# Summing layer 0's modulation by products with ones, moving a step's activations ahead of copies, and giving half-size weights their own small buffers

## The chip, the cores and the metric

One Trainium2 chip, one of its cores. The metric is the device time of one execution in microseconds (us). The kernel before takes 1404.36 us (median of 3 runs).

## The reference, cut to what matters

Two layers run over 512 positions of 2048 features. Each begins with a modulation that comes from the conditioning vector `c` alone, and with a wide projection of the modulated, normalised activations:

```python
c_act = jax.nn.silu(c)
for l in range(2):
    mod = c_act @ w_ada[l] + b_ada[l]            # 2048 x 6144
    shift, scale, gate = jnp.split(mod, 3, axis=-1)
    h = _layernorm(x) * (1.0 + scale[:, None, :]) + shift[:, None, :]
    p = h @ w_in[l]                              # 2048 x 3904
    u_f, z_f, cq, ckv, k_r, z_a = jnp.split(p, split_pts, axis=-1)
    # Fourier mixing of u_f, attention from cq, ckv, k_r, gates from z_f, z_a
    y = jnp.concatenate([y_f, y_a], axis=-1) @ w_out[l]
    x = _layernorm(DEEPNORM_ALPHA * x + gate[:, None, :] * y, ln_g[l], ln_b[l])
```

## The kernel before, in words

Every large product is split into a high and a low part of each operand (`split`: a cast on ScalarE, ACT, at L146, a subtraction on VectorE, DVE, at L147) and runs as three TensorE products (`mm3`, L150 to L152).

**Modulation.** `ada` goes over the rows of `w_ada`: a tile is loaded (L211), and DVE multiplies it by the conditioning values, one value for each partition, and adds it into `acc` (L244, L246). What is left is a sum over the 128 partitions. `finish` does it: each 128 x 128 block of `acc` is transposed on TensorE (L259, plain float32, against the identity), DVE sums along the free dimension (L260), and `ada_finish` adds the bias into `modT` (L220). `ada` is called 14 times in the two layers: six for the shift and scale of layer 0, two for its gate, six for layer 1. A block whose width is at most 512 has two halves in `acc`, and each half is transposed by itself. `finish` runs some units of weights later (`DL0`, `DLY`) or at the next step (`finish_late`).

**Layer 0's projection in steps.** All of `w_ada` would have to come before the first product, so layer 0 is cut into five steps of 1, 2, 3, 4 and 6 blocks of 128 features (`SZ`). A step needs only the shift and scale of its own blocks. In a step `make_h` modulates each block (an activation on ACT at L362, then `split`), and eight column groups follow (`k_group`, in the order of `FIRST`: UA, UB, CQ, CKV, two of ZF, two of ZA). UA keeps its own four PSUM banks (`pa`) over all steps. The other seven share the four banks of `pm`: in the first step their results are copied to SBUF sums by ACT (L1118), in later steps added to them by DVE (L1120). A bank is free for the next group when that is done. `finish` takes its banks from `pm` too: two for four or more blocks.

**Weights.** `Stream` loads ahead of use, up to four units, and converts two units ahead. A unit is two blocks of rows by up to 512 columns (512 KB), or one block where a step has an odd number (steps one and three, eight units each). `dense` gives every unit one of the three `wr` buffers (4 KB for each partition). The `t2` pool has nine buffers of 2 KB for each partition, for the modulated activations, rotary tables and other short-lived tiles. The loads are issued by the SP queue.

**Order.** The program is written in the order in which it should run, and a scheduler lays out each engine's queue: of the instructions that are ready by its own estimate, the one that stands first in the program goes first. On the chip each queue then runs in that order. `tc.high_priority(offset=n)` counts the instructions of a block as standing n places earlier. It moves nothing past its operands.

Of the kernel before, what the change touches and what calls it, by code (L numbers as in the profile page):

```python
# [9 lines left out]
F32 = mybir.dt.float32  # L10
# [3 lines left out]
ALU = mybir.AluOpType  # L14
AX = mybir.AxisListType
# [67 lines left out]
def trunk_kernel(ctx: ExitStack, tc: tile.TileContext, x, c, positions, w_ada, b_ada, w_in, q_norm,  # L83
# [8 lines left out]

    DL0, DLY = 2, 3

    KO = 2

    NE, HA = 5, 2
# [29 lines left out]
    def wraw(shape):  # L127
        return wrp.tile(shape, F32, tag="wr", name=nm("wr"))
# [4 lines left out]
    def sm(n, tag):  # L133
        return smp.tile([P, n], F32, tag=tag, name=nm(tag), bufs=4 if tag in ('mx', 'ssum') else 2)
# [4 lines left out]
    def pm():  # L139
        return psm.tile([P, 512], F32, tag="pm", name=nm("pm"))  # L140
# [36 lines left out]
    GP.dma_start(odd, odds)  # L177
    identr = const.tile([P, P], F32R, name="identr")
    V.tensor_copy(identr, ident)
    mhalf = const.tile([P, 4], F32, name="mhalf")  # L180
    V.memset(mhalf, -0.5)
    cact = const.tile([P, NK], F32, name="cact")
# [50 lines left out]
    def ada(l, pieces, cols, tiles=None):  # L233

        w = sum(n for _, n in pieces)
        nr = 1024 // w
        two = 2 if w <= 512 else 1
        acc = acp.tile([P, 1024], F32, tag="acc", name=nm("acc"))[:, :two * w].rearrange("p (a n) -> p a n", a=two)
        for r0 in range(0, NK, nr):
            t = tiles[r0 // nr] if tiles else ada_load(l, r0, nr, pieces)  # L240
            for r in range(r0, r0 + nr):
                a = acc[:, r % two]
                if r < two:
                    V.tensor_scalar(a, t[:, r - r0], cact[:, r:r + 1], None, op0=ALU.mult)  # L244
                else:
                    V.scalar_tensor_tensor(out=a, in0=t[:, r - r0], scalar=cact[:, r:r + 1], in1=a,  # L246
                                           op0=ALU.mult, op1=ALU.add)
            if r0 + nr < NK:
                yield

        def finish():
            red = sm(8, 'red')
            for i in range(0, w // P, 4 // two):
                ps = pm()
                n = min(4 // two, w // P - i)
                for j in range(n):
                    for a in range(two):
                        o = (j * two + a) * P
                        PE.transpose(out=ps[:, o:o + P], in_=acc[:, a, (i + j) * P:(i + j + 1) * P], identity=ident)  # L259
                V.tensor_reduce(red[:, i:i + n], ps[:, :n * two * P].rearrange("p (j q) -> p j q", j=n),  # L260
                                axis=AX.X, op=ALU.add)
            ada_finish(l, red[:, :w // P], *cols)
            if cols[0] == 40:
                ps = pm()
                PE.transpose(out=ps[0:16, 0:P], in_=modT[l][:, 32:48], identity=ident)
                row = t2([16, P])
                A.copy(row, ps[0:16, 0:P])
                SP.dma_start(gated[l:l + 1, :].rearrange("l (j q) -> (l j) q", q=P), row)

        late.append([DL0 if l == 0 and pieces[0][0] == SZ[0] * P else DLY, finish])  # L270
        yield
# [97 lines left out]

    def dense(src, row0, col0, n, nr=2):  # L370
        def load():
            t = wraw([P, nr, n])
            SP.dma_start(t, src[row0:row0 + nr * P, col0:col0 + n].rearrange("(r p) c -> p r c", p=P))
            return t

        def conv(t):
            h, l = big([P, nr, n]), big([P, nr, n])
            split(h, l, t)
            return h, l
        return Unit(load, conv)  # L380
# [273 lines left out]
    for l in range(DEPTH):  # L654
# [430 lines left out]
        if l == 0:  # L1085

            for step, (k0, nk) in enumerate(STEPS):
                final = k0 + nk == NK
                if step > 0:
                    finish_late()  # L1090
                for k in range(k0, k0 + nk) if step else ():
                    h[k] = make_h(0, xT[k // 2][:, k % 2], k)
                if final:
                    cw, dt = fourier_weights(0)
                left = [0 if final else float(sum(NK // (1024 // (256 * n)) for n in chunks(STEPS[step + 1][1])))]
                pace = left[0] / (8.0 * len(pairs(k0, nk)) * LEADS[step])

                def k_group(g, banks, work=lambda: None):
                    n = g[1]
                    k00, k01 = (0, NK) if g == UA else (k0, k0 + nk)  # L1100
                    for k, nr in pairs(k0, nk):
                        w = st.next()
                        p_ = min(pace, left[0])
                        left[0] -= p_
                        bg_step(p_ if p_ > 0 else ZL if final else ZP)
                        if g in ZF or g in ZA:
                            fm_half(banks, w, h, k, k == k00, k + nr == k01)
                        else:
                            tm_half(banks, w, h, k, n, k == k00, k + nr == k01)
                        work()  # L1110
                    if g == UA:
                        return banks
                    if k0 == 0:
                        sums[g] = [big([P, 2, n], F32) for _ in range(2)]
                    s_ = [sums[g][tb // 2][:, tb % 2] for tb in range(NT)]
                    for tb in range(NT):
                        if k0 == 0:
                            A.copy(s_[tb], banks[tb][:, :n])  # L1118
                        else:
                            V.tensor_tensor(s_[tb], s_[tb], banks[tb][:, :n], op=ALU.add)  # L1120
                    return s_

                if step == 0:
                    keep = [pa() for _ in range(NT)]
                if not final:
                    for i, g in enumerate(FIRST):
                        k_group(g, keep if g == UA else [pm() for _ in range(NT)])
                        if step == 0 and i == 3:
                            cos_t, sin_t = rotary_tables()
                    continue  # L1130

                def pas():
                    return [pa() for _ in range(NT)]

                def pieces(gen, then=iter(())):
                    def run():
                        next(then, None)
                        for _ in range(2):
                            next(gen, None)
                    return run  # L1140

                fa = fourier(0, folded(k_group(UA, keep)))
                pq = k_group(CQ, [pm() for _ in range(NT)])
                pkv = k_group(CKV, pas(), pieces(fa))
                lq = latent_q(pq)
                next(lq)
                ub = k_group(UB, pas(), pieces(fa, lq))
                drain(fa)
                lkv = latent_kv(pkv)
                next(lkv)  # L1150
                fb = fourier(1, folded(ub))
                for i, g in enumerate(ZF):
                    zs = k_group(g, pas(), pieces(fb, lkv))
                    silu(zs, zs)
                    if i == 0:
                        gate_f(0, zs)
                drain(fb)
                gate_f(1, zs)
                rq = rotary_queries(RN0)
                for i, g in enumerate(ZA):  # L1160
                    zs = k_group(g, pas(), runner(rq) if i else lambda: None)
                    silu(zs, zs)
                    spill(i, zs)
                    if i == 0:
                        next(rq)
        else:
            unfolded(first_group(), 0)
            st.ahead(4, UAH)
            with tc.issue_after(hold[0]):
                banks = fm_group(ada=G0)  # L1170
            unfolded(banks, H)
            cw, nq, dt = folded_constants(1)
            st.ahead(4, 2)
            fb = fourier_folded(u_pass())
            unfolded(fm_group(runner(fb, FW)), H + 4)
            drain(fb)
            gt = gates()
            lq = latent_q(tm_group(CQ, runner(gt)))
            drain(gt)
            next(lq)  # L1180
            lkv = latent_kv(tm_group(CKV, runner(lq), G1))
            next(lkv)
            rq = rotary_queries(1)

            def last():
                next(lkv, None)
                next(rq, None)

            next(rq)
            unfolded(fm_group(last, G1), 4)  # L1190
            drain(lkv)
# [160 lines left out]
```

## Time and profile before

| | us |
|---|---|
| median of 3 runs (lowest, highest) | 1404.36 (1404.01, 1406.08) |
| the profiled execution | 1404.26 |
| its span, first to last instruction | 1402.5 |
| TensorE busy | 1344.3 |
| VectorE busy | 1015.6 |
| ScalarE busy | 579.6 |

The span is the profiled time from the first instruction to the last. The 1.8 us around it belong to the time but not to any instruction. PE is TensorE's products, PEld its weight loads, which run beside the products. A queue with a q (SPq) is the issuing side of an engine. Products are pipelined: a record of 0.39 us is followed by the next one after about 0.23 us when nothing holds it.

### The profile page before, as it was taken

The page shows a single profiled execution, that of the slowest core. Times are in us where ns is not written, and L with a number is a line of the kernel's source. Part 1 is how long each engine was busy: PE and PEld are TensorE (multiplying, and loading weights), DVE is VectorE, ACT ScalarE, POOL GpSimd, SP SyncE. Part 2 cuts the span into 40 slices and gives each one's busy share as a digit, 9 for nine tenths or more (in the row PEclk, how much of TensorE's full clock was granted, in tenths as well). Part 3 has the DMA queues.
Part 4 walks back from the last instruction along what each step waited for, and adds up shares of the span by engine and source line. Part 5 has one row for each costly group of instructions (what it writes and reads, how often), then busy time and mean ns, then how long its engine had stood idle before and what let it go on. Part 6 is the DMA issues. An engine that isn't in the chain of part 4 may idle for free. (4 is left out here: it accounts for less than half of the span.)

```text
span 1402.5 us, 18691 instructions
## 1 busy us (share of the span) xinstructions
PE 1344.3 (96%) x6949; PEld 1141.2 (81%) x6949; DVE 1015.6 (72%) x1670; ACT 579.6 (41%) x1052; POOL 55.5 (4%) x82
## 2 busy tenths in 40 slices
PE   4899999999999999999988999998999999999996
PEld 3688888787888888788877888887898888888885
DVE  7899999849978986658588748567655576642448
ACT  6722332224437776112167524323234677721210
POOL 1000000000000000000030001011000000000001
PEclk9999999999999999999998999999999999999998
DMA  9988898824764444968336435369444221263323
GB/s 288 299 293 300 271 349 286 306 76 122 211 206 140 157 128 161 317 199 283 105 145 203 161 96 166 105 205 367 152 119 121 74 67 54 80 236 105 91 60 120
DMA packets 134546, 253.24 MB, mean 181 GB/s; under 512 B 19308, under 2 KB 50168, under 8 KB 134456
## 3 DMA queue, kind: packets, MB, share of 16 engines
q1 hardware_dynamic: 127416, 228.73, 50.1%
q0 software_dynamic: 7040, 23.34, 4.9%
q8 instruction: 54, 0.88, 0.3%
q14 instruction: 36, 0.29, 0.1%
HBM read 237.32 MB, written 14.70 MB: 180 GB/s over the span
## 5 line engine op out<-in xcount | busy, mean ns | idle before, releaser
L150 PE MATMUL pa<-b,b 128*128 128x512 f32 (+4 forms) x1432 | 537.4, 377 | 11.6 <-ACT b L146 5.5
L151 PE MATMUL pa<-b,b 128*128 128x512 f32 (+4 forms) x1432 | 535.9, 375 | 4.3 <-DVE ln_v L187 4.3
L152 PE MATMUL pa<-b,b 128*128 128x512 f32 (+4 forms) x1432 | 534.5, 374 | 1.9 <-DVE b L147 1.9
L146 ACT CAST b<-wr 128x1024 fp32r<-128x1024 f32 (+3 forms) x184 | 180.0, 988 | 356.1 <-PE pa L152 181.1
L150 PEld LDWEIGHTS pa<-b,b 128*128 128x128 f32 x1432 | 271.2, 190 | 59.7 <-ACT b L146 9.2
L151 PEld LDWEIGHTS pa<-b,b 128*128 128x128 f32 x1432 | 272.1, 190 | 48.1 <-DVE ln_v L187 4.6
L152 PEld LDWEIGHTS pa<-b,b 128*128 128x128 f32 x1432 | 271.5, 190 | 48.2 <-DVE b L147 2.9
L147 DVE TENSOR_TENSOR b<-wr,b 128x1024 fp32r<-128x1024 f32 (+3 forms) x184 | 208.1, 1141 | 136.5 <-PE pa L151 84.7
L246 DVE SCALAR_TENSOR_TENSOR acc<-ada,cact,acc 128x1024 f32<-128x1024 f32 (+2 forms) x193 | 227.2, 1184 | 23.1 <-DMA ada<-in_w_ada_dram 21.2
L150 PE MATMUL pm<-b,b 128*128 128x512 f32 (+3 forms) x594 | 201.7, 341 | 1.2 <-ACT b L146 0.8
L151 PE MATMUL pm<-b,b 128*128 128x512 f32 (+3 forms) x594 | 197.2, 333 | 0.0
L152 PE MATMUL pm<-b,b 128*128 128x512 f32 (+3 forms) x594 | 197.0, 333 | 0.0
L150 PEld LDWEIGHTS pm<-b,b 128*128 128x128 f32 x594 | 111.7, 189 | 17.8 <-ACT b L146 2.7
L151 PEld LDWEIGHTS pm<-b,b 128*128 128x128 f32 x594 | 112.3, 189 | 10.5
L152 PEld LDWEIGHTS pm<-b,b 128*128 128x128 f32 x594 | 112.2, 189 | 10.4
L146 ACT CAST b<-pm 128x512 fp32r<-128x512 f32 (+4 forms) x110 | 54.9, 530 | 72.6 <-PE pm L800 17.8
L147 DVE TENSOR_TENSOR b<-pm,b 128x512 fp32r<-128x512 f32 (+4 forms) x110 | 64.1, 610 | 23.6 <-ACT b L146 23.0
L1120 DVE TENSOR_TENSOR b<-b,pm 128x512 f32<-128x512 f32 (+1 forms) x88 | 55.5, 656 | 4.5 <-PE pm L152 4.1
L146 ACT CAST b<-t 128x512 fp32r<-128x512 f32 (+1 forms) x73 | 35.9, 525 | 31.4 <-PE pm L151 9.5
L1039 DVE TENSOR_REDUCE mx<-pa 128x1 f32<-128x512 f32 x64 | 42.9, 684 | 5.3 <-PE pa L1037 4.7
L1044 ACT ACTIVATE t<-t,ssum 128x512 f32<-128x512 f32 x64 | 45.9, 735 | 1.2 <-DVE ssum L1043 1.2
L1042 ACT ACTIVATE t<-pa,mx 128x512 f32<-128x512 f32 x64 | 44.0, 693 | 4.6 <-DVE mx L1039 4.5
(186 smaller groups left out, 1120.7 us busy)
## 6 DMA issues: line engine op xcount, KB each, us to landing
wr<-in_w_in_dram SPq DMA_DIRECT2D x105, 512.0 KB, 4.6
ada<-in_w_ada_dram SPq DMA_DIRECT2D x96, 512.0 KB, 5.3
wr<-in_w_out_dram SPq DMA_DIRECT2D x64, 512.0 KB, 4.1
ada<-in_w_ada_dram SPq DMA_DIRECT2D x96, 256.0 KB, 4.9
ada<-in_w_ada_dram POOLq DMA_DIRECT2D x32, 512.0 KB, 5.4
b<-in_x_dram SPq DMA_DIRECT2D x16, 512.0 KB, 6.3
ada<-in_w_ada_dram SPq DMA_DIRECT2D x32, 192.0 KB, 5.3
wr<-in_w_q_b_dram SPq DMA_DIRECT2D x48, 128.0 KB, 3.0
```

What stands on the lines that cost most here:

```text
L146: A.copy(hi, src)
L147: V.tensor_tensor(lo, src, f(hi), op=ALU.subtract)
L150: PE.matmul(o, lh, rh, start=first, stop=False)
L151: PE.matmul(o, lh, rl, start=False, stop=False)
L152: PE.matmul(o, ll, rh, start=False, stop=last)
L246: V.scalar_tensor_tensor(out=a, in0=t[:, r - r0], scalar=cact[:, r:r + 1], in1=a, op0=ALU.mult, op1=ALU.add)
L1039: V.reduce_max(mx, ps, axis=AX.X, negate=True)
L1042: A.activation(e, ps, AF.Exp, bias=mx, accum_out=ssum)
L1044: A.activation(e, e, AF.Copy, scale=ssum)
L1120: V.tensor_tensor(s_[tb], s_[tb], banks[tb][:, :n], op=ALU.add)
```

## The change

It has five edits.

1. `finish` uses no transposes and no reduction. Each block of `acc` is the stationary operand of a plain float32 product with a column of ones (`onec`, 128 x 1), two halves accumulate in PSUM, and `ada_finish` reads the sums from there. All 14 calls use it, in one PSUM bank each.
2. A unit of one row block goes into a `t2` buffer and not a `wr` buffer.
3. The `make_h` calls of a step stand 250 places earlier for the scheduler (`HP`).
4. In the first step, every second copy of the sums of the four ZF and ZA groups is on DVE and not on ACT (eight copies).
5. The column of ones is set once at the start.

```diff
+    HP = 250
...
+    onec = const.tile([P, 1], F32, name="onec")
+    V.memset(onec, 1.0)
...
         def finish():
-            red = sm(8, 'red')
-            for i in range(0, w // P, 4 // two):
-                ps = pm()
-                n = min(4 // two, w // P - i)
-                for j in range(n):
-                    for a in range(two):
-                        o = (j * two + a) * P
-                        PE.transpose(out=ps[:, o:o + P], in_=acc[:, a, (i + j) * P:(i + j + 1) * P], identity=ident)
-                V.tensor_reduce(red[:, i:i + n], ps[:, :n * two * P].rearrange("p (j q) -> p j q", j=n),
-                                axis=AX.X, op=ALU.add)
-            ada_finish(l, red[:, :w // P], *cols)
+            ps = pm()
+            for j in range(w // P):
+                for a in range(two):
+                    PE.matmul(ps[:, j:j + 1], acc[:, a, j * P:(j + 1) * P], onec, start=a == 0, stop=a == two - 1)
+            ada_finish(l, ps[:, :w // P], *cols)
...
-            t = wraw([P, nr, n])
+            t = wraw([P, nr, n]) if nr > 1 else t2([P, nr, n])
...
-                for k in range(k0, k0 + nk) if step else ():
-                    h[k] = make_h(0, xT[k // 2][:, k % 2], k)
+                with tc.high_priority(offset=HP):
+                    for k in range(k0, k0 + nk) if step else ():
+                        h[k] = make_h(0, xT[k // 2][:, k % 2], k)
...
                         if k0 == 0:
-                            A.copy(s_[tb], banks[tb][:, :n])
+                            if tb % 2 and (g in ZF or g in ZA):
+                                V.tensor_copy(s_[tb], banks[tb][:, :n])
+                            else:
+                                A.copy(s_[tb], banks[tb][:, :n])
```

## Rows read from the trace of the kernel before

**Rows 1.** The page's first part: busy us, share, instructions of each engine.

```profile
PE 1344.3 (96%) x6949; PEld 1141.2 (81%) x6949; DVE 1015.6 (72%) x1670; ACT 579.6 (41%) x1052; POOL 55.5 (4%) x82
```

**Rows 2.** Windows: stretch, its length, each engine's busy us, clock, DMA share, GB/s.

```profile
20.00:40.00 20.00, 16.25 (x89) 14.21 (x90) 18.39 (x42) 17.69 (x33) 0.17 (x1) 1.00 0.86 264
40.00:60.00 20.00, 16.56 (x78) 12.73 (x77) 14.75 (x22) 17.27 (x33) 0.00 (x0) 1.00 0.93 308
60.00:80.00 20.00, 18.63 (x90) 15.60 (x89) 19.51 (x26) 6.20 (x7) 0.00 (x0) 1.00 0.99 342
...
62.00:290.00 228.00, 227.84 (x1056) 190.70 (x1057) 213.79 (x262) 63.53 (x81) 2.95 (x5) 1.00 0.86 292
```

**Rows 3.** Timeline of PE, steps one to two: start us, us, instruction, idle before.

```profile
30.66 0.50 PE L150 MATMUL pa<-b,b 128*128 128x512 f32 x1 [1.58 <-ACT b L146]
...
46.28 0.30 PE L259 MATMUL pm<-ident,acc 128*128 128x128 f32 x1 [0.87 <-DVE acc L246]
46.85 0.98 PE L259 MATMUL pm<-ident,acc 128*128 128x128 f32 x7 [0.27 <-DVE acc L246]
...
54.03 0.50 PE L150 MATMUL pm<-b,b 128*128 128x512 f32 x1 [0.39 <-ACT b L1118]
...
58.91 0.50 PE L150 MATMUL pa<-b,b 128*128 128x512 f32 x1 [1.85 <-ACT b L146]
...
62.16 0.50 PE L152 MATMUL pa<-b,b 128*128 128x512 f32 x1 [1.37 <-DVE b L147]
```

**Rows 4.** Timeline of ACT around the start of step two.

```profile
50.07 0.82 ACT L362 ACTIVATE t<-xT,modT 128x512 f32<-128x512 f32 x1
...
56.24 2.09 ACT L1118 COPY b<-pm 128x512 f32<-128x512 f32 x4
58.15 1.23 ACT L146 CAST b<-t 128x512 fp32r<-128x512 f32 x2
```

**Rows 5.** Timeline of DVE: the modulation of steps one and two.

```profile
27.68 0.69 DVE L260 TENSOR_REDUCE red<-pm 128x2 f32<-128x512 f32 x1 [0.92 <-PE pm L259]
28.29 0.68 DVE L147 TENSOR_TENSOR b<-wr,b 128x512 fp32r<-128x512 f32 x1
28.89 0.16 DVE L220 TENSOR_TENSOR modT<-red,vecT 128x2 f32<-128x2 f32 x1
...
47.84 1.28 DVE L260 TENSOR_REDUCE red<-pm 128x2 f32<-128x512 f32 x2
...
49.64 0.16 DVE L220 TENSOR_TENSOR modT<-red,vecT 128x4 f32<-128x4 f32 x1
...
61.41 1.29 DVE L147 TENSOR_TENSOR b<-t,b 128x512 fp32r<-128x512 f32 x2
```

**Rows 6.** Groups by line: count, busy us, mean ns of one, idle before.

```profile
L260 DVE TENSOR_REDUCE red<-pm 128x4 f32<-128x512 f32 (+2 forms) x27 | 17.4, 675 | 3.6 <-PE pm L259 3.5
...
L259 PEld LDWEIGHTS pm<-ident,acc 128*128 128x128 f32 x106 | 12.5, 141 | 3.2 <-ACT b L1118 1.3 <-DVE acc L246 0.5
...
L1118 ACT COPY b<-pm 128x512 f32<-128x512 f32 (+1 forms) x28 | 14.6, 583 | 3.3 <-PE pm L152 2.9
...
L1120 DVE TENSOR_TENSOR b<-b,pm 128x512 f32<-128x512 f32 (+1 forms) x88 | 55.5, 656 | 4.5 <-PE pm L152 4.1
```

**Rows 7.** Timeline of PE: plain float32 products, six in the code at L554.

```profile
839.83 3.59 PE L554 MATMUL pm<-b,b 128*128 128x512 f32 x8
```

**Rows 8.** Timeline of PEld: weight loads of the same products, later in the same stretch.

```profile
843.88 0.30 PEld L554 LDWEIGHTS pm<-b,b 128*128 128x128 f32 x2 [0.19 <-PE pa L152]
```

**Rows 9.** Lines of that source: count of products, ns (min/median/max), first and last start.

```profile
L554 PE MATMUL pm<-b,b x12: 590/593/668, 839.8 to 845.3; 128*128 128x512 f32 x12
```

**Rows 10.** Timeline of the SP queue's issues.

```profile
19.78 0.43 SPq L211 DMA_DIRECT2D ada<-in_w_ada_dram  x1
25.21 0.33 SPq L373 DMA_DIRECT2D wr<-in_w_in_dram  x1
```

**Rows 11.** Waits from 36 to 64 us: total us, times, longest.

```profile
DVE acc L246 <- DMA ada<-in_w_ada_dram: 5.4, 6, 1.7
```

## The prediction

> **What bounds the kernel now.** I read the page's totals first, then the windows, then the timelines of the engines around layer 0's first steps, and then the rows of the instructions that are removed and added. TensorE is the bound: it is busy for 1344.3 of 1402.5 us, DVE for 1015.6 [rows 1]. The windows say where it is not. From 20 to 80 us it lacks 3.75, 3.44 and 1.37 us of each 20, and from 62 to 290 us, the rest of layer 0's steps, it lacks 0.16 of 228 us in all [rows 2]. DVE is at 94% in that stretch (213.79 of 228), but no product waits for it, so time taken off DVE there is worth nothing by itself, and time put on PE there is paid in full.
>
> The timeline of PE shows the one seam of the steps [rows 3]. The first product starts at 30.66. From 45 to 62 us PE stops five times: 0.87 and 0.27 us for `acc`, ahead of and between the transposes of step two's `finish`; 0.39 us for a copy of a sum that must free a `pm` bank; 1.85 us for the high part of step two's first `h`; 1.37 us for its low part. That is 4.75 us, and the windows from 40 to 80 us give 4.81 [rows 2]. The other engines say why the last two are so long. `modT` is there at 49.64 + 0.16 = 49.80 us [rows 5]. ACT does the first modulation at 50.07, but the cast to the high part only at 58.15, right behind the four copies of sums that start at 56.24, and DVE makes the low part at 61.41 [rows 4, 5]. So some 9 us go by in queues between operands that are ready and a cast of about 0.6 us.
>
> **Edit 1, the products with ones.** It removes 106 transposes, whose weight loads take 12.5 us together, 0.118 us each, and 27 reductions, 17.4 us of DVE [rows 6]. It adds 106 plain float32 products, as many as there were transposes, since each 128 x 128 block of `acc` is still the stationary operand. The moving side shrinks from 128 columns to one, but the time of a transpose here is its weight load, and that stays. The rows of a plain float32 product show more: the six products in the code at L554 leave twelve records [rows 9], and eight of them take 3.59 us, 0.449 each [rows 7], two passes of 512 columns at about 0.22. So each such product loads weights twice and streams its columns twice behind each load. With one column the streaming is next to nothing, and two weight loads are left. Two loads of L554 with no product between them take 0.30 us, 0.19 for the record of the second, so the second starts 0.11 us behind the first [rows 8]. I price a product with ones at two loads of 0.11 and a transpose at one: 0.11 us more each.
>
> No trace shows a one-column product, so the price is bounded from both sides: from below 0, if the second load hides; from above, if loads don't overlap at all and take the 0.19 us of their record, 2 x 0.19 - 0.118 = 0.26. I take 0.11, the value nearest to loads seen back to back. Of the 106, 12 lie in the first two steps and are counted there. The other 94 run where PE is full or where what follows waits for PE: 94 x 0.11 = **+10.3 us**. It has no cover: a full PE hides nothing, and a block's products follow each other with nothing wide between them to load behind.
>
> The 17.4 us of DVE come free mostly where nobody waits for them. In step one they count: the reduction of 0.69 us at 27.68 stands ahead of `modT` [rows 5], and the first product waits for what `modT` feeds [rows 3]. The four products with ones end 4 x 0.11 = 0.4 us later than the transposes, the reduction goes, and the subtraction of 0.68 us at 28.29 still contends for DVE: **-0.5 us**, between +0.4 and -0.8.
>
> **Edits 3 and 4, the seam.** With `make_h` 250 places ahead, ACT does the modulation and the cast as soon as `modT` is there, about 0.82 + 0.6 us for each of two blocks, some 3 us in all, and DVE's low parts run beside them. `h` is ready about 53 us and not 62, before PE has finished step one's groups. The 1.85 and the 1.37 us go. What is late next is ACT: those 3 us are queued ahead of copies that PE's banks wait for. Edit 4 pays for it: ACT loses eight copies of 0.58 us, 4.7 us, and DVE gets them at about 0.66 each, the price of an addition from PSUM of the same size [rows 6], 5.2 us. DVE has 5.25 us to spare from 40 to 60 us [rows 2], plus the 1.28 us of reductions at 47.84 [rows 5], so it holds them with little left over. But DVE runs in order, and in this stretch its additions into `acc` wait 5.4 us for loads, up to 1.7 at a time [rows 11]; a copy behind one of these keeps its bank. So I let the 0.39 us go, and count 0.5 us for such waits.
>
> The two stops for `acc` (1.14 us) are set by the arrival of `w_ada`, with DMA at a share of 0.93 [rows 2]. I keep half of them. The eight products cost 8 x 0.11 = 0.9 us in the same place. Sum for the seam: -1.85 - 1.37 - 0.39 - 0.57 + 0.5 + 0.9 = **-2.8 us**, and -0.5 us for pipeline ends: at each of the three stops that go, the record before it counts as busy some 0.16 us past the start of its successor. So **-3.3 us**. The bounds: 0 if all of it comes back as other waits, -5.3 if every stop goes, pipeline ends with it, and only the 0.9 stays.
>
> Beyond the first seam edit 3 has nothing to win: PE doesn't wait at a later step [rows 2].
>
> **Edit 2, the small buffers.** SP issues one `ada` load at 19.78 and nothing more until 25.21, where the next weight load has waited for a `wr` buffer [rows 10]; the `ada` loads behind it in SP's queue wait with it. Eight units in `t2` take that wait away, so `w_ada` for step two comes up to 5 us earlier. Against that, the three `wr` buffers are then free from the start, and the scheduler can load step two's first three units, 512 KB each, ahead of the last `w_ada` tiles. At 300 GB/s [rows 2] that is 5 us the other way. I count the two as **0**; both ends stand in the half that I keep of the `acc` stops, -0.6 to +4. No instruction's own time changes: the cast and the subtraction are the same.
>
> **Sum.** +10.3 - 0.5 - 3.3, and -0.5 for the first load of each of the other 12 calls, which can start behind a wide product and hide some 0.04 us there (an estimate: 0.23 from start to start of wide products, less the 0.19 of a load's record): +6.0. From the profiled execution's 1404.26 that is **1410 us**; the median of 1404.36 lies 0.1 above it, which changes nothing.
>
> **A rule beside the rows.** The Trainium skill, "FP8 and Floating Point Precision", section "TensorE Precision Notes", says that true float32 takes four passes through the array. The rows of L554 agree in the streaming, two records with two passes each; that the passes need two loads and not four is the rows' alone. Read as four loads, the rule gives rival 3.
>
> **Rivals.**
>
> 1. *The products are cheap (faster).* If a one-column product costs PE no more than the transpose did, because the second load runs while the first one's column passes, the +10.3 and +0.9 fall away and the gains stay: -0.5 - 4.2 = -4.7, 1399.6 us. For it speaks that only one column is streamed; against it that two bare loads of this kind start 0.11 us apart [rows 8] and that the transposes, whose stream is short too, are no faster than their loads [rows 6]. It decides from a price under 0.03 us for each product.
> 2. *The seam doesn't close (slower still).* `w_ada` comes later since three large units go first, or step-three units hold the `t2` buffers that `make_h` needs; PE stops for `acc` or for `h` as long as before. Then +10.3 + 0.9 and nothing back but the start: 1404.26 + 11 = 1415 us. For it: DMA is nearly full there [rows 2, 11]. Against it: SP's 5 us of waiting go [rows 10].
> 3. *Four loads for each product.* 3 x 0.11 = 0.33 more each, 94 x 0.33 + 8 x 0.33 = 33.7, less 4.7: 1433 us. Against it: twelve records for six products, not 24 [rows 9].
> 4. *Half and half.* A price near 0.06, or a better seam and a better start: +1 to +2, 1402 to 1407 us, no change that can be told.
>
> **How the numbers follow.** A measurement of this kernel can tell about 0.2%, 2.8 us, from no change. My forecast (1410, its own range 1406 to 1413) has 0.52; rival 1 0.16, rival 2 0.15, rival 3 0.04, rival 4 0.13. The time is that of the forecast. The range runs from rival 1's edge to a little past rival 2: 1400 to 1416. Leaving out rival 3 and the outer halves of rivals 1 and 2, it holds about 0.8. Slower by over 0.2% (past 1407.2) takes five sixths of the forecast and rivals 2 and 3: 0.63. Within 0.2%: the rest of the forecast and rival 4 without its edge, 0.20. Faster: rival 1 and that edge, 0.17.
>
> **What the new profile would show.** Right: 212 weight loads and 212 records at the line of the new product, back to back about 0.11 us apart; no reduction; PE's span from one `finish` product to the next wide one about twice what it was; step two's high parts at ACT within 3 us of `modT`; no stop of PE over 1 us from 50 to 64. Wrong: 106 records, or two records inside the time of one transpose (rival 1); stops for `acc`, or for `h` behind a full `t2`, in the seam (rival 2); four records each (rival 3). A change of layer 1's stretch beyond the products would be a surprise: only two of the 14 calls run there.

## The result and the profile after

The changed kernel takes 1411.51 us (median of 6 runs, 1408.79 to 1413.79) against 1405.22 for the kernel before, timed beside it (6 runs, 1401.40 to 1407.37): a ratio of 1.0051, with a 95% interval of 1.0037 to 1.0065. It is slower by 6 to 7 us. A second comparison gives 1411.74 to 1405.67, 1.0049 (1.0033 to 1.0065). The profiled execution took 1413.79, with a span of 1412.0.

First the page's totals and the windows of the changed kernel (first profile), with the columns of [rows 1, 2].

```profile
PE 1357.5 (96%) x7055; PEld 1156.2 (82%) x7055; DVE 1005.0 (71%) x1652; ACT 575.9 (41%) x1044; POOL 55.5 (4%) x82
...
40.00:60.00 20.00, 18.69 (x80) 15.25 (x79) 16.47 (x32) 13.02 (x25) 0.00 (x0) 0.83 0.68 225
60.00:80.00 20.00, 19.96 (x96) 16.84 (x95) 20.00 (x26) 6.06 (x7) 0.00 (x0) 1.00 0.97 321
80.00:100.00 20.00, 17.90 (x81) 14.38 (x82) 19.62 (x27) 1.57 (x2) 0.00 (x0) 1.00 0.96 324
62.00:290.00 228.00, 225.86 (x1055) 188.44 (x1054) 209.78 (x253) 62.29 (x80) 2.93 (x5) 1.00 0.86 291
```

PE and PEld have 106 records more. From 40 to 60 us PE lacks 1.31 us in place of 3.44, but from 80 to 100 it now lacks 2.10, in a stretch where it lacked nothing (0.16 in the 228 us of [rows 2]). The clock of 0.83 is taken up in the last section.

The instructions that read or write `onec`: count, ns (min/median/max), first and last start, forms.

```profile
L259 PEld LDWEIGHTS pm<-onec,acc x212: 186/192/338, 26.8 to 1242.1; 128*128 128x128 f32 x106
L259 PE MATMUL pm<-onec,acc x212: 164/250/353, 27.0 to 1242.1; 128*128 128x1 f32 x106
```

The 106 products leave 212 loads and 212 products. The PE timelines of one call in both kernels, first before, then after (start, us, instruction, count), give the price of each:

```profile
199.03 1.04 PE L259 MATMUL pm<-ident,acc 128*128 128x128 f32 x8
199.82 0.39 PE L150 MATMUL pm<-b,b 128*128 128x320 f32 x1
```

```profile
202.85 1.84 PE L259 MATMUL pm<-onec,acc 128*128 128x1 f32 x16
204.55 0.40 PE L152 MATMUL pm<-b,b 128*128 128x320 f32 x1
```

From the first of them to the product behind them PE needed 0.79 us for eight transposes and needs 1.70 for eight products: 0.099 against 0.213 each, two loads of 0.106 on average. No other undisturbed call of 16 records is shorter.

The PE timeline of the seam, to be laid beside [rows 3]:

```profile
30.30 0.50 PE L152 MATMUL pa<-b,b 128*128 128x512 f32 x1 [0.45 <-ACT b L148]
...
45.84 0.35 PE L259 MATMUL pm<-onec,acc 128*128 128x1 f32 x2 [0.79 <-DVE acc L250]
...
46.83 2.15 PE L259 MATMUL pm<-onec,acc 128*128 128x1 f32 x14
48.84 0.77 PE L152 MATMUL pm<-b,b 128*128 128x512 f32 x1
49.41 0.63 PE L153 MATMUL pm<-b,b 128*128 128x512 f32 x1
...
59.81 0.50 PE L152 MATMUL pa<-b,b 128*128 128x512 f32 x1 [0.51 <-ACT b L148]
...
81.37 0.47 PE L152 MATMUL pm<-b,b 128*128 128x512 f32 x1 [1.41 <-DVE b L1122]
...
87.75 0.47 PE L152 MATMUL pm<-b,b 128*128 128x512 f32 x1 [0.66 <-DVE b L1122]
```

Of the five stops two are left, 0.79 us for `acc` and 0.51 for the high part of `h`, 1.30 in place of 4.75. Two new ones, 1.41 and 0.66 us, stand 20 us later: there PE waits until DVE has added a sum out of a `pm` bank (L1122).

DVE's timeline shows where these begin (L250 is the addition into `acc`, L1118 the copy that edit 4 gave to DVE, L224 writes `modT`):

```profile
49.02 0.16 DVE L224 TENSOR_TENSOR modT<-pm,vecT 128x4 f32<-128x4 f32 x1 [0.33 <-PE pm L259]
...
50.50 0.69 DVE L1118 COPY b<-pm 128x512 f32<-128x512 f32 x1 [0.58 <-PE pm L154]
51.11 0.22 DVE L592 TENSOR_SCALAR cos_t<-cos_t 128x128 f32<-128x128 f32 x1
53.06 0.69 DVE L1118 COPY b<-pm 128x512 f32<-128x512 f32 x1 [1.74 <-PE pm L154]
53.67 1.01 DVE L250 SCALAR_TENSOR_TENSOR acc<-ada,cact,acc 128x768 f32<-128x768 f32 x1
...
62.73 1.01 DVE L250 SCALAR_TENSOR_TENSOR acc<-ada,cact,acc 128x768 f32<-128x768 f32 x1
```

Between 50 and 62.7 us one addition into `acc` runs, at 53.67, where the kernel before starts five:

```profile
52.41 1.02 DVE L246 SCALAR_TENSOR_TENSOR acc<-ada,cact,acc 128x768 f32<-128x768 f32 x1 [1.69 <-DMA ada<-in_w_ada_dram]
...
55.07 2.08 DVE L246 SCALAR_TENSOR_TENSOR acc<-ada,cact,acc 128x768 f32<-128x768 f32 x2 [0.49 <-DMA ada<-in_w_ada_dram]
...
59.21 1.02 DVE L246 SCALAR_TENSOR_TENSOR acc<-ada,cact,acc 128x768 f32<-128x768 f32 x1 [0.93 <-DMA ada<-in_w_ada_dram]
60.48 1.02 DVE L246 SCALAR_TENSOR_TENSOR acc<-ada,cact,acc 128x768 f32<-128x768 f32 x1 [0.25 <-DMA ada<-in_w_ada_dram]
```

The work is missing later, and DVE is then full, 20.00 of 20 us from 60 to 80. Two of the copies wait for PE's groups here, 0.58 and 1.74 us, but that is mostly the low clock of this profile: in the second profile of the same kernel, with the full clock, the copies wait 0.4 us in all, two additions start between 50 and 60 us, and the stops are the same, 1.41 and 0.65 us. So it is the 5.5 us that eight copies take which push the additions back, more than their waiting.

ACT's timeline, which answers to [rows 4] (L360 is the modulation, L1120 a copy of a sum, L148 the cast):

```profile
49.57 0.81 ACT L360 ACTIVATE t<-xT,modT 128x512 f32<-128x512 f32 x1 [0.94 <-DVE modT L224]
50.29 0.80 ACT L360 ACTIVATE t<-b,modT 128x512 f32<-128x512 f32 x1
51.78 0.59 ACT L1120 COPY b<-pm 128x512 f32<-128x512 f32 x1 [0.69 <-PE pm L154]
52.27 1.05 ACT L148 CAST b<-wr 128x1024 fp32r<-128x1024 f32 x1
...
58.65 0.59 ACT L1120 COPY b<-pm 128x512 f32<-128x512 f32 x1 [0.72 <-PE pm L154]
59.13 1.14 ACT L148 CAST b<-t 128x512 fp32r<-128x512 f32 x2
```

Both modulations run right behind `modT`. The cast doesn't: it still stands behind five copies and two casts of weights, 10 us after `modT`. In the second profile, with the full clock, it stands behind the same seven, 7 us after `modT` (48.87):

```profile
56.01 1.14 ACT L148 CAST b<-t 128x512 fp32r<-128x512 f32 x2
```

### The profile page after: what moved, and what is told of

It reads as the page before. It is cut to its first block, busy times and chain, and to the rows that moved or that the text cites. A ratio compares the mean times of both kernels' runs of the same rounds, so it can differ in the third digit from the quotient of the medians.

```text
span 1412.0 us, 18870 instructions
## 1 busy us (share of the span) xinstructions
PE 1357.5 (96%) x7055; PEld 1156.2 (82%) x7055; DVE 1005.0 (71%) x1652; ACT 575.9 (41%) x1044; POOL 55.5 (4%) x82
## 5 line engine op out<-in xcount | busy, mean ns | idle before, releaser
L148 ACT CAST b<-wr 128x1024 fp32r<-128x1024 f32 (+1 forms) x168 | 169.8, 1023 | 339.5 <-PE pa L154 181.8
L149 DVE TENSOR_TENSOR b<-wr,b 128x1024 fp32r<-128x1024 f32 (+1 forms) x168 | 198.0, 1187 | 147.3 <-PE pa L153 84.5
L250 DVE SCALAR_TENSOR_TENSOR acc<-ada,cact,acc 128x1024 f32<-128x1024 f32 (+2 forms) x193 | 227.3, 1185 | 13.0 <-DMA ada<-in_w_ada_dram 11.1
L153 PEld LDWEIGHTS pm<-b,b 128*128 128x128 f32 x594 | 113.0, 190 | 10.7
L148 ACT CAST b<-pm 128x512 fp32r<-128x512 f32 (+4 forms) x110 | 54.7, 531 | 71.5 <-PE pm L798 17.9
L149 DVE TENSOR_TENSOR b<-pm,b 128x512 fp32r<-128x512 f32 (+4 forms) x110 | 63.8, 610 | 23.0 <-ACT b L148 22.5
L148 ACT CAST b<-t 128x512 fp32r<-128x512 f32 (+2 forms) x89 | 45.5, 539 | 54.6 <-PE pm L154 13.8
L1122 DVE TENSOR_TENSOR b<-b,pm 128x512 f32<-128x512 f32 (+1 forms) x88 | 55.5, 659 | 4.8 <-PE pm L154 4.5
L149 DVE TENSOR_TENSOR b<-t,b 128x512 fp32r<-128x512 f32 (+2 forms) x89 | 50.1, 584 | 9.5 <-ACT b L148 9.3
```

The lines of the kernel that those rows point to most:

```text
L148: A.copy(hi, src)
L149: V.tensor_tensor(lo, src, f(hi), op=ALU.subtract)
L153: PE.matmul(o, lh, rl, start=False, stop=False)
```

## Experiments

Each is named by what it contains. Edit 1 is the products with ones, edit 2 the small buffers, edit 3 the priority of `make_h`, edit 4 DVE's copies. Ratios are to the kernel before, run beside it.

### What a product with ones costs

**Edit 1 alone, and edits 2 to 4 without it.** The first adds to the kernel before

```
+            ps = pm()
+            for j in range(w // P):
+                for a in range(two):
+                    PE.matmul(ps[:, j:j + 1], acc[:, a, j * P:(j + 1) * P], onec, start=a == 0, stop=a == two - 1)
+            ada_finish(l, ps[:, :w // P], *cols)
```

for the transposes and the reductions; the second is the changed kernel with these lines taken back.

> The kernel before with edit 1 alone. By the price of the products: 12.4 us more of PE, plus 1 to 4 us of half-rate clock where a run of them follows a stop or is 32 loads long, less 1 to 2 us of reductions that nobody waits for any more: 1415 to 1420. The rival (the other edits cost) expects 1404 to 1408.

> Edits 2, 3 and 4 with the transposes and reductions of the kernel before. If the products with ones are what costs (12.4 us more of PE, and about 4 us of wide products at the 1.2 GHz level behind two of their runs), this kernel is faster than the one before by what the other edits give: 2 to 6 us, 1399 to 1403. PE's clock stays at 1.00 from 40 to 60 and from 680 to 700 us. The rival, that the moved copies, order and buffers are what costs, expects 1407 or more here.

Edit 1 alone: 1416.69 us, 1.0088 (1.0067 to 1.0110). Edits 2 to 4: 1404.38, 0.9995 (0.9982 to 1.0007). So edit 1 makes the loss; but edits 2 to 4 don't gain the 2 to 6 us that were expected of them. By itself edit 1 costs 12.4 us, near the 11 that rival 2 counts for the products with an open seam, and its PE does wait there as long as before (2.3 for `acc`, 1.9 and 0.7 for `h`, 4.9 us). Beside the products the other edits give back 5 us (1.0088 to 1.0051), alone less than 1; that the two don't add up is only just outside what the intervals leave open.

**The same products with one load each.** The last two additions write a rounded tile, and `onec` is rounded and two columns wide; so these sums are rounded. All else is the changed kernel.

```
+            if r0 + nr == NK:
+                last = big([P, two, w])
...
-                    V.scalar_tensor_tensor(out=a, ...
+                    V.scalar_tensor_tensor(out=last[:, r % two] if r >= NK - two else a, ...
...
+                    PE.matmul(ps[:, 2 * j:2 * j + 2], last[:, a, j * P:(j + 1) * P], onec, ...
```

> All edits, but the last additions round the sums to the reduced float32 format, in which a product loads its weights once; the column of ones is two wide. The modulation is summed from rounded values, so the computation is less exact. If the price is one more load for each product, the line of the products has 106 records at about 0.11 us, 12 us of PE come back, PE's clock stays at 1.00 from 40 to 60 and from 680 to 700 us, and the time is 1396 to 1401. If a product with ones costs what it does for another reason (its place, its short stream), 1408 or more.

1401.55 us, 0.9977 (0.9966 to 0.9988). Its rows of `onec`:

```profile
L261 PEld LDWEIGHTS pm<-onec,b x106: 186/192/337, 28.1 to 1231.7; 128*128 128x128 f32 x106
L261 PE MATMUL pm<-onec,b x106: 165/250/353, 28.2 to 1231.7; 128*128 128x2 f32 x106
```

That is 0.5 us above the expected range. One load per product and, but for a buffer for the rounded sums, the same kernel: from 1.0049 to 0.9977, 10 us, which is 106 second loads at some 0.1 us. This is the cleanest test of the price.

**Columns, and a second time.** In one kernel `onec` is read as 64 columns, of which one is used; in another every product is done a second time into columns that nobody reads.

```
+                    PE.matmul(ps[:, 64 * j:64 * j + 64], acc[:, a, j * P:(j + 1) * P], onec.broadcast_to([P, 64]), ...
```

> All edits, with 64 columns of ones and not one: the same 212 loads, each product streams 64 columns, and one column of each result is read. If only loads count, the products take 0.106 us for each record as before, and 1410 to 1413 us if the clock falls in the same two places. If the low clock behind the runs near 48 and 690 us comes with products of one column, it stays at 1.00 there and 3 to 4 us come back: 1406 to 1409.

```
+            for j in range(w // P):
+                for a in range(two):
+                    PE.matmul(ps[:, 8 + j:9 + j], acc[:, a, j * P:(j + 1) * P], onec, start=a == 0, stop=a == two - 1)
```

> All edits, and every product with ones a second time into unused columns of the bank (212 more loads). By loads of 0.106 us: 22.5 us more, 1434. If the clock falls behind a run of 32 such loads wherever one is, as it did near 690 us, it falls behind about eleven more runs at 1.5 to 3 us each: 1450 to 1465. If the products were hidden in part, less than 15 us more: under 1427.

64 columns: 1411.02 us, 1.0045 (1.0029 to 1.0061), as with one, though its profile has the full clock in both places. Up to 64 columns cost nothing behind two loads that the time shows. Twice: 1455.90, 1.0368 (1.0341 to 1.0395), 44 us above the changed kernel, where 212 loads at 0.106 make 22.5. The rest is TensorE's clock, by the mean granted clock of the two profiles, first the doubled kernel, then the changed one:

```profile
core 0: 1459.7 us, clock 0.971
```

```profile
core 0: 1412.0 us, clock 0.987
```

The clock missing from 1 is 0.029 x 1459.7 = 42 us of work in the one and 0.013 x 1412.0 = 18 in the other, so 24 us more. Together 46, for a difference of 48 between these spans.

**The changed kernel and the 64 columns again**, each timed once more, since the first profile of the changed kernel had a low clock at two places.

> The changed kernel once more, beside the one with 64 columns of ones on the same chip: 1410 to 1413. In its first profile the clock was at the 1.2 GHz level for 6.8 us from 47.7 and for 3.4 us from 689.4. If that belongs to the kernel and not to one execution, it is there again in at least the second place.

> 64 columns of ones once more, beside the changed kernel on the same chip. If the low clock behind the one-column products costs what the first profile shows, about 4 us, this one is 2 to 4 us under the changed kernel. If it costs nothing that can be measured, the two agree within 1.5 us.

1411.74 us, 1.0049 (1.0033 to 1.0065), and 1411.97, 1.0043 (1.0029 to 1.0058): the same. In this profile of the changed kernel the clock is 1.00 from 48 to 54.5 us and from 684 to 700, so the low clock was expected in the second place and is in neither; the span is 1408.2 in place of 1412.0.

### What the other edits are worth

**Edit 2 alone; edits 3 and 4; edits 2 and 3.** All keep transposes and reductions.

```
+            t = wraw([P, nr, n]) if nr > 1 else t2([P, nr, n])
```

> The kernel before with edit 2 alone. My prediction counted it at nothing: 1403 to 1407, with SP's silence from 19.8 to 25.2 us gone and PE's stops for the modulation of step two within 1 us of what they were. If early loads of later units hold up the modulation's weights, or small units hold the buffers that the modulated activations need, 1408 or more and a longer stop near 46 us.

```
+                with tc.high_priority(offset=HP):
...
+                            if tb % 2 and (g in ZF or g in ZA):
+                                V.tensor_copy(s_[tb], banks[tb][:, :n])
```

> The kernel before with edits 3 and 4 alone (order of the modulation, eight copies on DVE). The seam's stops for the high and the low part go: 3.2 to 4.5 us less, less what comes back as waits for PSUM banks that DVE frees: 1400 to 1404. The rival: DVE frees banks late, 1405 or more, with stops for the additions to the sums from 75 to 95 us.

```
-                            if tb % 2 and (g in ZF or g in ZA):
-                                V.tensor_copy(s_[tb], banks[tb][:, :n])
```

> Edits 2 and 3 alone: transposes and reductions as before, all copies of the first step's sums on ACT. In the kernel with edits 2 to 4 PE stops for 3.2 us between 76 and 88 us, for banks that DVE frees. Theory: the eight copies on DVE wait for PE in front of additions into acc whose weights have landed, and these additions are then late and stand between the additions that free banks. Then the stops from 76 to 90 us go (under 0.6 us in all) and 1 to 4 us are won: 1400 to 1403. Rival: PE only comes earlier into a stretch in which DVE is full anyhow; then the stops stay at 2 us or more, and the time at 1403 to 1406.

Edit 2: 1403.07 us, 0.9985 (0.9971 to 0.9999). Edits 3 and 4: 1405.30, 1.0008 (0.9995 to 1.0020), the rival's time, with the rival's stops of 1.42 and 0.65 us. Edits 2 and 3: 1400.62, 0.9969 (0.9956 to 0.9983), which beats both kernels of the case. Against edits 2 to 4 that is 0.9969 to 0.9995, so edit 4 costs 3.6 us here, by the two intervals some 1 to 6. The windows without it (edits 2 and 3):

```profile
40.00:60.00 20.00, 17.73 (x82) 13.52 (x81) 18.44 (x33) 18.90 (x37) 0.00 (x0) 1.00 0.76 255
60.00:80.00 20.00, 20.00 (x98) 17.11 (x97) 19.24 (x26) 5.64 (x6) 0.00 (x0) 1.00 0.93 316
80.00:100.00 20.00, 20.00 (x93) 16.61 (x92) 19.37 (x27) 2.70 (x5) 0.00 (x0) 1.00 0.89 317
```

and with it (edits 2 to 4), with what PE waits for from 44 to 95 us:

```profile
40.00:60.00 20.00, 19.43 (x89) 14.75 (x88) 19.81 (x37) 15.70 (x30) 0.00 (x0) 1.00 0.74 250
60.00:80.00 20.00, 18.22 (x88) 15.29 (x87) 20.00 (x26) 4.21 (x4) 0.00 (x0) 1.00 0.98 332
...
PE pm L152 <- DVE b L1126: 2.4, 3, 1.4
PE pa L152 <- ACT b L148: 0.5, 1, 0.5
```

The stops for DVE's additions, 2.1 us or more, are there in every kernel with edit 4 that was run, and gone without it here: edit 4 causes them. How it does is not quite the theory. With the copies DVE waits for nothing from 44 to 60 us and is busy for 19.81 of 20 from 40 on, so the copies don't hold it up by waiting for PE. They take the time themselves: from 51 to 60 us DVE starts one addition into `acc` with them and six without. In the seam itself the copies on DVE do win something, 0.5 us of stops in place of 2.3.

**Edits 1 to 3; and the one-load products with edits 2 and 3.** Each is a kernel above with edit 4 taken back in the same lines.

> The changed kernel without edit 4 (all copies on ACT), products with ones as in the change. If edit 4 cost 3 us of stops for banks here too, they go, and 1407 to 1410 comes out. If with the products the copies on DVE pay for themselves in the seam, 1411 or more.

> Products with ones that load their weights once (sums rounded to the reduced float32 format first, so less exact), edits 2 and 3, and all copies on ACT. The price of the second load and the bank stops from 76 to 90 us are both gone, and 17 us of reductions too: 1397 to 1401, at or a little under the 1400.6 of edits 2 and 3 with transposes. If the reductions on DVE had cost anything, clearly under it, 1397 or less.

With two loads: 1412.90 us, 1.0050 (1.0030 to 1.0070); 1407 to 1410 was expected, so this missed: no gain over the changed kernel's 1.0049. With one load: 1400.51, 0.9960 (0.9946 to 0.9975), against 0.9977 with edit 4, 2.4 us, a difference that the two intervals don't tell from none. It is the fastest kernel of the study, with the rounded sums; without them the fastest is edits 2 and 3. In the profile of the miss PE waits 1.0 us for the cast, 0.8 for `acc` and 0.7 for an addition of DVE, and the clock from 40 to 60 us is 0.91:

```profile
40.00:60.00 20.00, 18.17 (x85) 14.86 (x84) 15.86 (x29) 17.03 (x34) 0.00 (x0) 0.91 0.74 243
80.00:100.00 20.00, 19.25 (x90) 15.51 (x90) 19.09 (x27) 2.38 (x3) 0.00 (x0) 1.00 0.97 336
```

So the bank stop shrinks there but doesn't go. By time edit 4 costs 3.6 us beside transposes, 2.4 beside one load and nothing beside two, each known to some 3 us, so they don't contradict each other. The traces narrow it: from the first wide product to the start of the transposes or products with ones that finish step three's modulation PE needs 65.48 us with edit 4 and 63.49 without it beside transposes, 65.38 and 64.44 beside one load, and 65.57 and 66.28 beside two. In the last kernel eight wide products in a row start 0.43 us apart in place of 0.23, under the low clock, which is 1.6 us; without it edit 4 would cost some 0.9 us there too (an estimate). So up to there it costs some 1 to 2 us in all three.

## Why the prediction held, step by step

The forecast was 1410 us, measured are 1411.5 and 1411.7, inside the forecast's own range. The terms, against the second profile of the changed kernel (span 5.7 us above that of before), which has no low clock in the seam:

| term | predicted, us | measured, us |
|---|---|---|
| start: first wide product | -0.5 | -0.25 (30.41 for 30.66), first profile -0.36 |
| the 94 products of later calls | +10.3 | (1.70 - 0.79) / 8 x 94 = +10.7 |
| first load hidden in 12 calls | -0.5 | 0, contained in the row above |
| seam, its eight products included | -3.3 | -0.7, to the start of step three's products with ones (96.90 to 95.98, less the start) |
| PE waits for DVE at 589 us | not counted | -2.1 |
| everything else | 0 | -1.9 (what is left of 5.7) |

**The price of the products was right**, and it decides the sign. Two loads of L554 that start 0.11 us apart [rows 8] gave it; 212 records at 0.106 and the one-load kernel's 10 us bear it out. That puts rival 1 (cheap products) and rival 3 (four loads, 424 records) out. The -0.5 for hidden first loads was not there: 16 and 32 records take 1.70 and 3.49 us, so a run hides some 0.09 us of its first load, but 8 and 16 transposes take 0.79 and 1.66 and hide about as much. The Trainium skill ("FP8 and Floating Point Precision", "TensorE Precision Notes") gives true float32 four passes through the array; the rows of L554 agree, and no run here counts the passes of a product with ones, since 64 columns cost what one does.

**The seam was the step that failed, in two places.** "ACT does the modulation and the cast as soon as `modT` is there" holds for the modulation alone. The cast ran 7 us after `modT` (8 before the change, and 10 in the profile with the low clock), behind copies and casts of weights in ACT's order. What shortened the stop was edit 4, which leaves fewer copies ahead of it: with edits 2 and 3 PE waits 1.4 us for the cast, with edit 4 added 0.5. What keeps the cast back in ACT's order (a free buffer for `h` is one candidate) wasn't tried. And the 0.5 us counted for a copy behind a stalled DVE were 2.1 us, the other way round from what was argued: not a copy that waits behind an addition, but additions that come late because of the copies, and PE stops 20 to 30 us later for the additions that DVE then owes. The 5.25 us that DVE had "to spare" were mostly waits for `w_ada`, of work that still had to be done. With edits 2 and 3 the waits for loads are gone from 44 to 60 us (3.8 before), DVE is busy for 18.44 of 20 us from 40 to 60, and the 1.56 that are left don't hold 5.5 us of copies. The `acc` stops went from 1.14 to 0.79, where half of them was kept; with edit 2 and transposes they are gone. By stops alone: 4.75 go, 1.30 and 2.07 remain or come, and 0.9 for eight products, -0.5; the milestones give -0.7. (The prediction's bound of -5.3 for the seam leaves out the 0.9 that it says stays; with it the bound is -4.4.)

**Edit 2 was counted at nothing** because two effects were set against each other. SP's issues show that the first came: the silence from 19.78 to 25.21 [rows 10] is gone in the changed kernel.

```profile
19.68 2.69 SPq L215 DMA_DIRECT2D ada<-in_w_ada_dram  x5
22.90 2.64 SPq L371 DMA_DIRECT2D t<-in_w_in_dram  x4
25.96 0.38 SPq L215 DMA_DIRECT2D ada<-in_w_ada_dram  x1
```

Five `ada` loads go out in place of one. Alone the edit gains 2 us (interval 0.1 to 4), where the bounds let it gain 0.6 at most.

**DVE's 17.4 us of reductions were not all free beyond step one.** In the kernel before, PE's waits from 570 to 620 us are one row (total, times, longest):

```profile
PE pa L150 <- DVE b L1223: 2.1, 2, 1.6
```

Neither profile of the changed kernel has a wait there. Among kernels that keep the reductions it is 2.1 us (edits 2 to 4), 1.8 (edit 2), 1.4 (edits 2 and 3) and 0.5 (edits 3 and 4); among those without them none (edit 1, both one-load kernels), 0.2 (edits 1 to 3) and 1.0 (64 columns). The prediction looked for waits on DVE in layer 0's steps alone [rows 2], and held that time taken off DVE is worth nothing by itself; at this place it may be worth 1 to 2 us. That the reductions are the cause is argued from these rows; no run took out the reductions and nothing else. The pair that comes nearest, one-load products against transposes, both with edits 2 and 3, was expected to show any price of the reductions clearly and differs by 1.3 us (0.9960 and 0.9969), within the intervals.

Of the last 1.9 us, 1.2 lie between the calls at 1042 and 1232 us: from start to start 190.27 us before and 190.02 after, though the first of the two calls has 0.9 us more of products. So there the price was not paid, against the prediction's "no cover"; the first profile gives the same. For the rest one profile of each kernel can't tell.

**Why the time came out right.** The seam gave 2.6 us less than forecast, the products cost 0.9 more and the start gave 0.25 less; the 2.1 at 589 us and the rest made up for them. The mechanism of the largest term and the sign were right; that the number is within 1.7 us is partly luck, since gains that were not counted made up for the seam. Of rival 2, the seam did stay half open, but not through `w_ada` or the `t2` buffers.

## What to carry to other kernels

Price a small product by its weight loads: where the stationary operand is as large as before, a reduction by products with ones costs at least what the transposes did, and in plain float32 twice that, with 64 columns as with one. Before giving an engine work for its idle time, ask what the idle time is: where it is a wait for loads, the work behind it is only put off, and an earlier load takes the room away. Here eight copies of 0.69 us cost PE 2 us of stops, some 20 us later, by pushing back the additions that feed the next step. And test parts separately: two of the four edits alone are 0.3% faster than the kernel before, the four together 0.5% slower.

## What of the hardware was not expected

TensorE's granted clock fell to 0.50, its 1.2 GHz level, at or behind runs of these products in some executions and not in others. Windows of the changed kernel, first profile, with the columns of [rows 2]:

```profile
48.00:54.50 6.50, 6.50 (x18) 5.28 (x19) 3.86 (x9) 3.72 (x7) 0.00 (x0) 0.50 0.50 171
689.00:693.00 4.00, 4.00 (x16) 3.38 (x16) 2.17 (x5) 0.00 (x0) 0.00 (x0) 0.57 0.07 6
```

The second profile of the same kernel:

```profile
48.00:54.50 6.50, 6.50 (x32) 5.46 (x33) 6.07 (x13) 5.62 (x10) 0.00 (x0) 1.00 0.51 179
```

In the first, the run of products with ones ends at 48.84, and the wide products behind it then start 0.43 us apart in place of 0.23; in the second, the same run is followed by the full clock, 32 records in the stretch in place of 18. With the products done twice most runs of them are followed by such a stretch, for example 9.5 and 13 us long:

```profile
50.50:60.00 9.50, 9.50 (x32) 8.34 (x33) 3.64 (x8) 3.63 (x7) 0.00 (x0) 0.50 0.25 82
719.50:732.50 13.00, 13.00 (x52) 12.12 (x52) 2.40 (x5) 0.00 (x0) 0.00 (x0) 0.50 0.11 34
```

PE counts as busy all the while; only the clock column and the records per stretch tell of it. Stretches of low clock are not new with these products: every kernel of the study has some, the kernel before from 736 to 747 us for one (clock 0.53), and edit 2 alone, which has no such product, has one behind its stop of 2.6 us at 58 us, where wide products start 0.43 us apart. Near 50 us it came in the profiles of edit 1 alone and edits 1 to 3 (0.91 from 40 to 60 us) and in neither profile with 64 columns. Mean clock and time go together, loosely, over the executions of one kernel, before as well: in the last comparison the kernel before had spans of 1398.0 and 1399.7 us at 0.993 and of 1405.1 and 1407.7 at 0.987, but also one of 1411.3 at 0.988. So two profiles of one kernel can differ by 4 us for this alone, and a single one must not be read to less than that. Whether the two-load products lower the clock more often than the transposes did, in the median, no comparison here settles.
